# A decoder step with matrix products in seven parts: reading PSUM sums between the products of an accumulation, and another order of the seven products

## The chip, the cores and the metric

The kernel runs on one core of one Trainium2 chip. The metric is the device time of one execution in microseconds; the time before is the median of three runs. One further execution was profiled, and every duration below that is not a run's time comes from it. TensorE does the matrix products (PE, with its weight loads as PEld), VectorE (DVE), ScalarE (ACT) and GpSimd (POOL) the element-wise work; SyncE (SP) and GpSimd issue the DMAs. Products end in PSUM, out of which VectorE and ScalarE read them.

## The reference

One inference step of a decoder layer for 1024 prompt tokens and 8 sample tokens (1032 columns), everything in float32: a projection into pooling and convolution branches, an output projection, cross attention over 256 memory tokens, and a SwiGLU, each added to the residual, and a last normalisation. What matters here is the SwiGLU, with D_MODEL 1024 and D_FF 2816:

```python
    h = rmsnorm(x, g_ffn)
    x = x + (jax.nn.silu(h @ w_gate) * (h @ w_up)) @ w_down
```

## The kernel before

Columns of activations are tokens, partitions are channels. D_FF is cut into 22 tiles of 128, which the code counts with `f` and which are called values 0 to 21 here. Each float32 operand is split into a high and a low float32r part, and each product runs three passes (`PASSES`: high by high, high by low, low by high).

**Gates and values.** For one value the kernel computes two results (gate and up) for two halves of the tokens (`TH` = 516 columns), over two halves of the 1024 input channels: a product of 2 x 2 by 2 x 2 blocks. It is done as seven block products instead of eight, by sums of blocks made beforehand on both sides. On the token side the seven operands A11, A12, A22, S1, S2, S3, S4 lie in SBUF, split, for the whole stage (`ab`, 14 buffers). On the weight side `gate_prep` splits the gate weights (`wG`), and `sums_prep` forms four differences and sums (`ta`, `tb`, L1266) of the raw weights (`gr`, two loads a value) and splits them and the up weights (`wTa`, `wTb`, `wU`). A split is a high part on ScalarE or GpSimd (L363, L365) and a low part on VectorE or GpSimd (L374). A block product is `product` (L1288): 4 channel tiles x 3 passes x 2 column pieces of 258 are 24 matmuls (L1307) into one PSUM buffer. Three buffers are used in turn: two wide ones of the tag `mm` (both column pieces under one read of 516 columns), and one narrow pair of the tag `ms` (two reads of 258).

The results are sums over several products. They are formed in SBUF, in the tile `su` of a value: `copy_sums` (L1326) copies a product out with ScalarE, `plus_sums` (L1322) adds one to a quarter of `su` with VectorE. `first_two`, `sixth` and `others` (L1373 to L1412) do this in the order A11, S2, A12, S3, S1, A22, S4; for the values 0 and 1 (`AHEAD` = 2) A11 and A12 come first, since their other weights come later. S1 is read twice. So a value has one copy by ScalarE and seven additions by VectorE. Between them stand `gated` (times the token factor `Rf`, SiLU, times `Rf`; L1348, L1355), `times_value` (gate times up) and, for every second value up to 15, `combine` (L1330), which forms the seven operands of the w_down product from two neighbouring values. These go to DRAM (`hb`); values 16 to 21 go to DRAM as they are (`hd`).

**The w_down product.** `down(u)` runs for 16 units: 4 quarters `c` of the first 16 values by 4 pairs `p` of output tiles, again as seven block products, of 2 channel tiles each: 12 matmuls into one PSUM buffer. The weights of a unit come by `dn_load` and `dn_prep` (raw `dr`, sums `dt`, split into `dV` for S1, S2, S3, A22 and `dW` for A11, A12, S4), the operands by `down_blocks` (`hs`, split into `hb`), four of the seven blocks of a quarter after the first by an accumulating DMA (L385, L392). The order is `DOWN_ORDER`, which decides too which blocks are loaded first. Each product is added by VectorE to one or two of six quarters of sums (four in `x2`, two in `pp`); in the first quarter two of these start as copies by ScalarE. `both` adds quarters to one another. A last stage (`last_down`, tiles `fd`, L1606) adds the values 16 to 21 and `final` normalises.

**The order of work.** The code lists tasks; `Program.order` places them on the engines once, when the program is built, by costs per engine, by the order in which they were listed, and by the number of buffers of each tag (3 `raw`, 2 `w`, 3 `scr`, 19 `op`, 2 `mm`, 2 `ms`). Each engine then works through its own list in that order, so an instruction that waits holds up all that stand behind it on that engine.

Of the kernel before, what the change touches and what calls it, by code (L numbers as in the profile page):

```python
# [11 lines left out]
ALU = mybir.AluOpType  # L12
# [61 lines left out]
DOWN_ORDER = (A11, S2, A12, S3, S1, A22, S4)  # L74
# [178 lines left out]
def hybrid_step_kernel(ctx: ExitStack, tc: tile.TileContext, io):  # L253
# [1034 lines left out]
    def product(w, cols, xs, steps=1):  # L1288
# [4 lines left out]
        state["products"] += 1  # L1293
        if i % 3 < 2:
# [8 lines left out]
        def emit(e, js):  # L1303
            for j in js:
                for p, (wi, xi) in enumerate(PASSES):
                    for c in range(2):
                        e.matmul(bank(c), w[:, wi, cols(j)], xs[0](j, xi)[:, c * TQ : (c + 1) * TQ],  # L1307
                                 start=j == 0 and p == 0, stop=j == nj - 1 and p == 2)
# [25 lines left out]
    def of_tokens(w, col, b, steps=1):  # L1334
        return product(w, lambda j: slice(col + j * P, col + (j + 1) * P),
                       (lambda j, p: block(b, j, p), [[bkey(b, j, p) for p in range(2)] for j in range(4)]), steps)
# [36 lines left out]
    def first_two(f, between=lambda: None):  # L1373
        G = gu_w[f][0]
        su[f] = op_buf(f"su{f}", (P, 4, TH))
        copy_sums(part(f, 1), (su[f], 1), of_tokens(G, 0, A11, 4 if f < AHEAD else 1))
        between()
        plus(f, 1, 0, of_tokens(G, 512, A12, 4 if f < AHEAD else 1))
# [5 lines left out]
    def others(f):  # L1384
# [6 lines left out]
        gated(f, 1)  # L1391
        if f < FIRST_LAST and f % 2 == 0:
            he[f] = scr(f"he{f}", (P, 2, TH))
        k, e = su[f], f - 1
        second = f < FIRST_LAST and f % 2
        times_value(f, 1)
        if second:
# [3 lines left out]
        plus(f, 2, 2, of_tokens(U, 0, S4))  # L1401
        times_value(f, 0)
        if second:
# [5 lines left out]
        else:  # L1409
            dma(lambda: hd[f - FIRST_LAST], lambda: su[f][:, 0:2].rearrange("p h n -> p (h n)"), 4 * P * T,  # L1410
                r=[(k, 0), (k, 1)], w=[("hd", f)])

# [60 lines left out]
    def down(u):  # L1473
        c, p = u // 4, u % 4
        W, V = dn_w.pop(u)
        if not c:
# [3 lines left out]
            both(p, 2, 2, 4, ALU.subtract)  # L1480

        def of_hidden(b, w, cols, wkeys):
            o = db[c, b]
            return product(w, cols, (lambda j, x: o[:, x, j], [[(o, 0), (o, 1)] + wkeys] * 2))

        def plain(b, col):
            W_part = [(W, x, 0 if col(1) < 512 else 1) for x in range(2)]
            return of_hidden(b, W, lambda j: slice(col(j), col(j) + P), W_part)

        def summed(b, q):  # L1490
            return of_hidden(b, V, lambda j: slice((2 * q + j) * P, (2 * q + j + 1) * P), [])
# [7 lines left out]
        first = plain(A11, lambda j: 2 * j * P)  # L1499
        into(3, first, True)  # L1500
        into(0, first)
        into(3, summed(S2, 2))
        into(0, plain(A12, lambda j: (2 * j + 1) * P))
        into(5, summed(S3, 3), True)
        into(4, summed(S1, 0))
        into(1, summed(A22, 1))
        if c == CHUNKS - 1:
# [279 lines left out]
```

## Time and profile before

| | us |
|---|---|
| median of three runs | 1253.48 (1253.13 to 1254.77) |
| the profiled execution | 1253.93 |
| its span, first to last instruction | 1252.2 |
| gates and values, within the span | 560 to 1001 |
| w_down, within the span | 1001 to 1171 |
| last stage, within the span | 1171 to the end |

The mean granted TensorE clock was 0.994. In the rows of the profile, a group or a timeline row has line, engine, operation, output tile <- input tiles with the buffer numbers left out, the shape, and the count. A number in brackets at the end of a timeline row is the idle time of that engine just before it, with the instruction that ended it. Matmul ends are modelled, so a row of TensorE reaches some tenths of a microsecond into the next one's start.

### The profile page before, as it was taken

The page shows a single profiled execution, that of the slowest core. Times are in us where ns is not written, and L with a number is a line of the kernel's source. Part 1 is how long each engine was busy: PE and PEld are TensorE (multiplying, and loading weights), DVE is VectorE, ACT ScalarE, POOL GpSimd, SP SyncE. Part 2 cuts the span into 40 slices and gives each one's busy share as a digit, 9 for nine tenths or more (in the row PEclk, how much of TensorE's full clock was granted, in tenths as well). Part 3 has the DMA queues.
Part 4 walks back from the last instruction along what each step waited for, and adds up shares of the span by engine and source line. Part 5 has one row for each costly group of instructions (what it writes and reads, how often), then busy time and mean ns, then how long its engine had stood idle before and what let it go on. Part 6 is the DMA issues. An engine that isn't in the chain of part 4 may idle for free.

```text
span 1252.2 us, 22041 instructions
## 1 busy us (share of the span) xinstructions
PE 1217.0 (97%) x8946; PEld 1191.6 (95%) x8946; DVE 928.5 (74%) x1548; ACT 516.3 (41%) x715; POOL 481.8 (38%) x428
## 2 busy tenths in 40 slices
PE   8999989999999999999999999999999999999997
PEld 7999977999999889989999999999999999999996
DVE  7899997756267785688878668776776887768644
ACT  6766755444224534452322222222322254423533
POOL 3587682322100112205241433133321667778301
PEclk9999999999999999999999999999999999999999
DMA  7445787437465764321323133313313597666812
GB/s 280 101 87 133 172 249 207 167 117 225 139 228 163 232 267 133 118 102 60 110 102 111 60 114 116 111 60 110 119 68 119 203 304 205 183 175 186 185 54 83
DMA packets 59877, 186.48 MB, mean 149 GB/s; under 512 B 8000, under 2 KB 11776, under 8 KB 58496
## 3 DMA queue, kind: packets, MB, share of 16 engines
q1 hardware_dynamic: 52288, 157.74, 35.8%
q0 software_dynamic: 7488, 27.34, 12.2%
q8 instruction: 70, 1.15, 0.4%
q14 instruction: 31, 0.25, 0.1%
HBM read 151.42 MB, written 33.64 MB: 148 GB/s over the span
## 4 chain that ended last, share of the span: by engine, by line
PE 49%; DVE 3%; DMA 1%; issue 1%; POOL 0%; ACT 0%; DVEq 0%; SPq 0%; ACTq 0%; POOLq 0%
PE pr L1307 44%; PE fd L1606 6%; DMA dr<-in_w_dn 1%; DVE hb L374 1%; DVE x L1322 1%; DMA hs<-hb 0%; DVE dW L374 0%; POOL dt L1448 0%; DVE su L1348 0%; DVE dV L374 0%; DVE pp L1330 0%; DVE x L1658 0%; DVE pp L1322 0%; DVE dt L1448 0%; PE fin_ps L1637 0%
## 5 line engine op out<-in xcount | busy, mean ns | idle before, releaser
L1322 DVE TENSOR_TENSOR su<-pr,su 128x258 f32<-128x258 f32 (+1 forms) x204 | 109.5, 559 | 78.1 <-PE pr L1307 74.6
L1307 PE MATMUL pr<-ab,wG 128*128 128x258 f32 x1056 | 136.1, 286 | 3.1 <-ACT wG L363 1.3
L1307 PEld LDWEIGHTS pr<-ab,wG 128*128 128x128 f32 x1056 | 131.5, 192 | 4.1 <-ACT wG L363 1.4
L1307 PE MATMUL pr<-ab,wTa 128*128 128x258 f32 x1056 | 133.5, 283 | 0.0
L1307 PE MATMUL pr<-ab,wTb 128*128 128x258 f32 x1056 | 130.9, 283 | 0.0
L1307 PEld LDWEIGHTS pr<-ab,wTa 128*128 128x128 f32 x1056 | 129.7, 189 | 0.0
L1307 PEld LDWEIGHTS pr<-ab,wTb 128*128 128x128 f32 x1056 | 128.8, 190 | 0.0
L471 PE MATMUL ps<-xop,w 128*128 128x344 f32 x720 | 113.9, 320 | 0.0
L471 PEld LDWEIGHTS ps<-xop,w 128*128 128x128 f32 x720 | 113.3, 188 | 0.0
L1307 PE MATMUL pr<-hb,dV 128*128 128x258 f32 x768 | 98.6, 284 | 2.9 <-DVE x L1322 2.2
L1307 PEld LDWEIGHTS pr<-hb,dV 128*128 128x128 f32 x768 | 95.0, 190 | 3.7 <-issue 1.2
L471 PE MATMUL ps<-xq,w 128*128 128x344 f32 x576 | 94.2, 321 | 0.0
L471 PE MATMUL po<-oo,w 128*128 128x344 f32 x576 | 91.0, 320 | 0.4 <-DVE oo L1080 0.4
L471 PEld LDWEIGHTS po<-oo,w 128*128 128x128 f32 x576 | 90.7, 188 | 0.7 <-DVE oo L1080 0.7
L471 PEld LDWEIGHTS ps<-xq,w 128*128 128x128 f32 x576 | 90.6, 188 | 0.1
L1322 DVE TENSOR_TENSOR x<-pr,x 128x516 f32<-128x516 f32 (+1 forms) x122 | 63.6, 556 | 21.9 <-PE pr L1307 20.3
L1307 PE MATMUL pr<-hb,dW 128*128 128x258 f32 x576 | 74.8, 283 | 3.2 <-DVE x L1322 1.8
L675 DVE SCALAR_TENSOR_TENSOR cacc<-glu,vec,cacc 128x511 f32<-128x511 f32 (+14 forms) x116 | 76.8, 744 | 0.0
L1307 PEld LDWEIGHTS pr<-hb,dW 128*128 128x128 f32 x576 | 71.5, 189 | 3.7 <-DVE x L1322 2.0
L1606 PE MATMUL fd<-ho,w 128*128 128x258 f32 x576 | 70.0, 283 | 0.8 <-DVE x L1322 0.8
L1606 PEld LDWEIGHTS fd<-ho,w 128*128 128x128 f32 x576 | 69.4, 189 | 1.0 <-ACT w L385 1.0
L1307 PE MATMUL pr<-ab,wU 128*128 128x258 f32 x528 | 67.4, 284 | 0.0
(328 smaller groups left out, 2317.4 us busy)
## 6 DMA issues: line engine op xcount, KB each, us to landing
gr<-in_w_gu SPq DMA_DIRECT2D x44, 512.0 KB, 3.4
hs<-hb SPq DMA_DIRECT2D x28, 516.0 KB, 3.5
hb<-su SPq DMA_DIRECT2D x8, 1032.0 KB, 4.6
dr<-in_w_dn SPq DMA_DIRECT2D x16, 512.0 KB, 7.0
hb<-hb POOLq DMA_DIRECT2D x12, 516.0 KB, 8.3
spcache_k<-in_cache_k SPq DMA_DIRECT2D x12, 512.0 KB, 3.7
raw<-in_w_in SPq DMA_DIRECT2D x10, 512.0 KB
w<-in_w_in POOLq DMA_DIRECT2D x9, 512.0 KB, 6.5
```

Of the source, the lines that this page charges most:

```text
L374: e.tensor_tensor(dst(1), src(), f32(dst(0)), ALU.subtract)
L471: e.matmul(ps[:, c, :CW], w[:, wi, cols], x[:, xi, c * CW : (c + 1) * CW], start=first and p == 0, stop=last and p == 2)
L675: e.scalar_tensor_tensor(acc[h][:, n:], src[:, : HALF - n], w, acc[h][:, n:], ALU.mult, ALU.add)
L1307: e.matmul(bank(c), w[:, wi, cols(j)], xs[0](j, xi)[:, c * TQ : (c + 1) * TQ], start=j == 0 and p == 0, stop=j == nj - 1 and p == 2)
L1322: from_sums(sums, "DVE", dve, lambda e, src, sl: e.tensor_tensor(as_banks(o(sl), src), src, as_banks(a(sl), src), ALU.add), [akey], [okey])
L1606: e.matmul(view(i), w[:, wi, col : col + P], hops[k][:, xi, lo + i * width // count : lo + (i + 1) * width // count], start=(k == 0 and p ...
```

## The change

Some sums are now formed in PSUM. `product` gets `onto`: the matmuls of a product go on adding into a buffer that holds an earlier product (`start=False`), after that buffer was read. A new function `seven` replaces `first_two`, `sixth` and `others` for the values 2 to 21. It runs A11, A12, S2, S1, S3, S4, A22. A11 is copied out by ScalarE; S2 goes onto it, and their sum is copied out; S3 goes onto that, and the sum is added to the copy of S1; A22 goes onto that, and this sum is one of the results as it stands, so VectorE multiplies it by `Rf` as it reads it. S4 goes onto S1. A12 alone keeps the narrow pair. So a value has three copies by ScalarE, three additions by VectorE and one multiplication out of PSUM. Each buffer is wanted again after one product in between. The combinations and stores of a value now follow its last product (`to_hidden`).

In `down` the same is done with S2 onto A11 and S4 onto S1, in the order A11, A12, S1, S2, S3, S4, A22. A subtraction of quarters at the start of each pair goes, `second_half` and the additions of the last quarter use other quarters, and the count of buffers is stepped over (`state["products"] += 1`) so that each buffer has two products between its uses.

```diff
-DOWN_ORDER = (A11, S2, A12, S3, S1, A22, S4)
+DOWN_ORDER = (A11, A12, S1, S2, S3, S4, A22)
...
-    def product(w, cols, xs, steps=1):
+    def product(w, cols, xs, steps=1, onto=None, narrow=None):
...
-        state["products"] += 1
-        if i % 3 < 2:
+        if onto is None and narrow is None:
+            state["products"] += 1
+            narrow = i % 3 == 2
+        if onto is not None:
+            sums = onto
+        elif not narrow:
...
-                                 start=j == 0 and p == 0, stop=j == nj - 1 and p == 2)
+                                 start=onto is None and j == 0 and p == 0, stop=j == nj - 1 and p == 2,
+                                 skip_group_check=onto is not None)
...
+    def seven(f):
+        G, U, Ta, Tb = gu_w[f]
+        su[f] = op_buf(f"su{f}", (P, 4, TH))
+        k = su[f]
+        one = of_tokens(G, 0, A11, narrow=False)
+        copy_sums(part(f, 0), (k, 0), one)
+        plus(f, 0, 0, of_tokens(G, 512, A12, narrow=True))
+        gated(f, 0)
+        of_tokens(Ta, 0, S2, onto=one)
+        copy_sums(part(f, 2), (k, 2), one)
+        two = of_tokens(Tb, 0, S1, narrow=False)
+        copy_sums(part(f, 3), (k, 3), two)
+        of_tokens(Ta, 512, S3, onto=one)
+        plus(f, 3, 3, one)
+        of_tokens(U, 0, S4, onto=two)
+        plus(f, 2, 2, two)
+        start_kept(f)
+        times_value(f, 0)
+        of_tokens(Tb, 512, A22, onto=one)
+        o = part(f, 1)
+        from_sums(one, "DVE", dve, lambda e, src, sl: e.tensor_tensor(
+            as_banks(o(sl), src), src, as_banks(Rf[:, TH + sl.start : TH + sl.stop], src), ALU.mult), RF, [(k, 1)])
+        add({"ACT": act(TH)}, lambda e: e.activation(o(), o(), AF.Silu), [(k, 1)], [(k, 1)], func=AF.Silu)
+        times(f, 1, lambda: Rf[:, TH:], RF)
+        times_value(f, 1)
+        to_hidden(f)
...
-            both(p, 2, 2, 4, ALU.subtract)
...
         first = plain(A11, lambda j: 2 * j * P)
+        into(0, first)
+        into(0, plain(A12, lambda j: (2 * j + 1) * P))
+        fifth = summed(S1, 0)
+        into(4, fifth)
+        summed(S2, 2, first)
         into(3, first, True)
-        into(0, first)
-        into(3, summed(S2, 2))
-        into(0, plain(A12, lambda j: (2 * j + 1) * P))
+        state["products"] += 1
         into(5, summed(S3, 3), True)
-        into(4, summed(S1, 0))
+        plain(S4, lambda j: 512 + j * P, fifth)
+        into(2, fifth)
+        state["products"] += 1
+        if c == CHUNKS - 1:
+            both(p, 2, 2, 3)
         into(1, summed(A22, 1))
...
-        both(p, 3, 3, 5)
-        both(p, 1, 1, 3)
+        both(p, 5, 3, 5)
+        both(p, 1, 1, 5)
         both(p, 3, 4, 5)
...
         if f < AHEAD:
             sixth(f)
+            others(f)
         else:
-            first_two(f, lambda: sixth(f))
-        others(f)
+            seven(f)
```

The orders on TensorE, VectorE, ScalarE, GpSimd and SP are the same up to value 1. VectorE's order within value 7 (in the rows, `su7` is this value's tile, `pr` a PSUM buffer, `wG8`, `wTb8`, `ta9`, `tb9` weights of the next two values), before, from the read of S2 to the second multiplication by `Rf`:

```order
L1322 TENSOR_TENSOR su7_6873<-pr52_6908,su7_6873 128x516
L1322 TENSOR_TENSOR su7_6873<-pr53_0_6939,su7_6873 128x258
L1322 TENSOR_TENSOR su7_6873<-pr53_1_6940,su7_6873 128x258
L1266 TENSOR_TENSOR ta9_6999<-gr9_1_6966 128x512
L1266 TENSOR_TENSOR ta9_6999<-tb9_6997,gr9_1_6966 128x512
L1322 TENSOR_TENSOR su7_6873<-pr54_6970,su7_6873 128x516
L1322 TENSOR_TENSOR su7_6873<-pr53_0_6939,su7_6873 128x258
L1322 TENSOR_TENSOR su7_6873<-pr53_1_6940,su7_6873 128x258
L1322 TENSOR_TENSOR su7_6873<-pr55_7002,su7_6873 128x516
L374 TENSOR_TENSOR wU8_7060<-gr8_1_6717,wU8_7060 128x512
L1348 TENSOR_TENSOR su7_6873<-su7_6873,Rf_5298 128x516
```

The same in the changed kernel, where `pr14_6772` holds A11 and then S2, S3 and A22, and `pr14_6870` S1 and then S4, from the split of wG8 on:

```order
L374 TENSOR_TENSOR wG8_6858<-gr8_0_6554,wG8_6858 128x1024
L374 TENSOR_TENSOR wTb8_6863<-tb8_6734,wTb8_6863 128x1024
L1354 TENSOR_TENSOR su7_6830<-su7_6830,Rf_5298 128x516
L1266 TENSOR_TENSOR tb9_6922<-gr9_1_6868,gr9_0_6770 128x512
L1266 TENSOR_TENSOR ta9_6924<-gr9_1_6868 128x512
L1266 TENSOR_TENSOR ta9_6924<-tb9_6922,gr9_1_6868 128x512
L1266 TENSOR_TENSOR tb9_6922<-gr9_0_6770,ta9_6924 128x512
L1328 TENSOR_TENSOR su7_6830<-pr14_6772,su7_6830 128x516
L1328 TENSOR_TENSOR su7_6830<-pr14_6870,su7_6830 128x516
L1354 TENSOR_TENSOR su7_6830<-su7_6830 128x516
L1445 TENSOR_TENSOR su7_6830<-pr14_6772,Rf_5298 128x516
```

Four reads of sums are left of seven, and the read of S3 (the row with `pr14_6772` and `su7` on both sides) stands behind the four differences and sums of value 9's weights, of which two stood on VectorE in value 7 before.

ScalarE's order around value 7 before (L1326 is the copy, L1355 SiLU, L363 high parts):

```order
L1326 ACTIVATE su7_6873<-pr49_6812 128x516
L363 ACTIVATE wTb8_6906<-tb8_6775 128x1024
L1355 ACTIVATE su7_6873<-su7_6873 128x516
L363 ACTIVATE wTa9_7028<-ta9_6999 128x1024
L363 ACTIVATE wU8_7060<-gr8_1_6717 128x512
L1355 ACTIVATE su7_6873<-su7_6873 128x516
```

And now (L1332 the copy, L1361 and L1447 SiLU):

```order
L1332 ACTIVATE su7_6830<-pr14_6772 128x516
L363 ACTIVATE wG8_6858<-gr8_0_6554 128x1024
L363 ACTIVATE wTb8_6863<-tb8_6734 128x1024
L1361 ACTIVATE su7_6830<-su7_6830 128x516
L1332 ACTIVATE su7_6830<-pr14_6772 128x516
L1332 ACTIVATE su7_6830<-pr14_6870 128x516
L363 ACTIVATE wU8_6977<-gr8_1_6653 128x512
L363 ACTIVATE wTa9_7009<-ta9_6924 128x1024
L1447 ACTIVATE su7_6830<-su7_6830 128x516
```

The copies of S2's and S1's sums have come in behind the first SiLU.

VectorE's order at the end of the first quarter of w_down before (`x2_3` and `pp1` hold sums of unit 3, `x2_0` of unit 4; `hb1_` are blocks of the second quarter):

```order
L1322 TENSOR_TENSOR x2_3_10456<-pr175_10586,x2_3_10456 128x516
L1322 TENSOR_TENSOR x2_3_10456<-pr176_0_10604,x2_3_10456 128x258
L1322 TENSOR_TENSOR x2_3_10456<-pr176_1_10605,x2_3_10456 128x258
L374 TENSOR_TENSOR dW4_10599<-dr4_10439,dW4_10599 128x256
L374 TENSOR_TENSOR hb1_3_10618<-hs1_3_10297,hb1_3_10618 128x1032
L374 TENSOR_TENSOR hb1_1_10636<-hs1_1_10358,hb1_1_10636 128x1032
L374 TENSOR_TENSOR hb1_2_10654<-hs1_2_10384,hb1_2_10654 128x1032
L1322 TENSOR_TENSOR x2_3_10456<-pr177_10623,x2_3_10456 128x516
L1322 TENSOR_TENSOR pp1_10193<-pr179_0_10659,pp1_10193 128x258
L1322 TENSOR_TENSOR x2_3_10456<-pr180_10680,x2_3_10456 128x516
L1322 TENSOR_TENSOR pp1_10193<-pr179_1_10660,pp1_10193 128x258
L1322 TENSOR_TENSOR x2_3_10456<-pr181_10698,x2_3_10456 128x516
```

And now:

```order
L1328 TENSOR_TENSOR x2_3_10288<-pr35_0_10393,x2_3_10288 128x258
L1328 TENSOR_TENSOR x2_3_10288<-pr35_1_10394,x2_3_10288 128x258
L1328 TENSOR_TENSOR x2_3_10288<-pr36_10413,x2_3_10288 128x516
L1328 TENSOR_TENSOR pp1_10025<-pr37_10432,pp1_10025 128x516
L374 TENSOR_TENSOR hb1_1_10461<-hs1_1_10234,hb1_1_10461 128x1032
L1487 TENSOR_TENSOR dt5_10410<-dt5_10410,dr5_10311 128x256
L1328 TENSOR_TENSOR x2_3_10288<-pr37_10432,x2_3_10288 128x516
L1487 TENSOR_TENSOR dt5_10410<-dr5_10311,dt5_10410 128x256
L374 TENSOR_TENSOR dW5_10515<-dr5_10311,dW5_10515 128x512
L1328 TENSOR_TENSOR x2_3_10288<-pr41_0_10501,x2_3_10288 128x258
L1328 TENSOR_TENSOR x2_3_10288<-pr41_1_10502,x2_3_10288 128x258
L1328 TENSOR_TENSOR x2_0_9863<-pr42_10523,x2_0_9863 128x516
```

Of the three splits of blocks between the reads one is left on VectorE; the two others stand on GpSimd.

42 lines of the change are left out of this document (19 added, 23 removed).

## Prediction

> **What bounds the kernel now.** I read the page first, then the chain of waits in order of time, then TensorE's timeline for its gaps, and last what stands in front of each gap. The page's first section:
>
> ```profile
> span 1252.2 us, 22041 instructions
> PE 1217.0 (97%) x8946; PEld 1191.6 (95%) x8946; DVE 928.5 (74%) x1548; ACT 516.3 (41%) x715; POOL 481.8 (38%) x428
> ```
>
> TensorE is busy for 97% of the span, so the change cannot earn what it takes off VectorE; it can earn only TensorE's gaps, in the stages it touches. In the chain of waits in order of time (start, length, work) the stage of gates and values is one piece:
>
> ```profile
> 560.15 428.60 PE pr L1307 x3548
> ...
> 1001.26 6.05 PE pr L1307 x48
> ...
> 1171.11 38.55 PE fd L1606 x318
> ```
>
> For 428.60 us TensorE waits for nothing. The gaps lie from the last value to the first `fd` product. TensorE's timeline shows them in brackets at the row's end, with the instruction that ended each:
>
> ```profile
> 1001.26 1.69 PE L1307 MATMUL pr<-hb,dW 128*128 128x258 f32 x12 [0.95 <-DVE su L1322]
> ...
> 1007.98 3.19 PE L1307 MATMUL pr<-hb,dV 128*128 128x258 f32 x24 [0.69 <-ACT pp L1326]
> ...
> 1043.50 3.15 PE L1307 MATMUL pr<-hb,dW 128*128 128x258 f32 x24 [1.80 <-DVE x L1322]
> ...
> 1070.82 4.57 PE L1307 MATMUL pr<-hb,dV 128*128 128x258 f32 x36 [1.04 <-DVE x L1322]
> ...
> 1085.91 3.13 PE L1307 MATMUL pr<-hb,dW 128*128 128x258 f32 x24 [0.41 <-DVE pp L1322]
> ...
> 1134.51 3.07 PE L1307 MATMUL pr<-hb,dV 128*128 128x258 f32 x23 [0.52 <-DVE x L1322]
> ...
> 1154.15 4.60 PE L1307 MATMUL pr<-hb,dV 128*128 128x258 f32 x36 [0.64 <-DVE x L1322]
> ...
> 1171.11 38.55 PE L1606 MATMUL fd<-ho,w 128*128 128x258 f32 x318 [0.78 <-DVE x L1322]
> ```
>
> Together 0.95 + 0.69 + 1.80 + 1.04 + 0.41 + 0.52 + 0.64 + 0.78 = 6.83 us. Every releaser is an instruction that reads a sum out of PSUM: TensorE wants the buffer back. That is all there is to win, 0.5% of the span. The two stages by windows (length, busy time of PE, PEld, DVE, ACT, POOL, then clock, DMA share, GB/s):
>
> ```profile
> 560.15:988.76 428.61, 428.61 (x3550) 428.61 (x3551) 322.06 (x456) 116.02 (x157) 142.72 (x92) 1.00 0.27 96
> 1001.20:1171.10 169.90, 163.97 (x1344) 162.56 (x1345) 135.95 (x215) 77.24 (x98) 130.19 (x113) 1.00 0.78 212
> ```
>
> The first row gives 428.61 / 3550 x 24 = 2.90 us for a product of gates and values, and the second 163.97 / 1344 x 12 = 1.46 us for one of the w_down stage. The clock is full in both.
>
> **Gates and values (values 2 to 21).** The number of matmuls stays. Reads of sums by VectorE go from seven to four for a value and ScalarE's copies from one to three; one of VectorE's four now multiplies, and replaces a multiplication of SBUF by SBUF. VectorE's price is in the page's fifth section (line, tiles, count, busy time, mean ns, then idle time before):
>
> ```profile
> L1322 DVE TENSOR_TENSOR su<-pr,su 128x258 f32<-128x258 f32 (+1 forms) x204 | 109.5, 559 | 78.1 <-PE pr L1307 74.6
> L1322 DVE TENSOR_TENSOR x<-pr,x 128x516 f32<-128x516 f32 (+1 forms) x122 | 63.6, 556 | 21.9 <-PE pr L1307 20.3
> ```
>
> VectorE already waits 74.6 us for TensorE in front of the first group, so time taken off it here brings nothing: this part's gain is 0. What it can cost is new waits. Before, a buffer was wanted again three products later, two products of cover. Now S2 goes onto the sum of A11, S3 onto that of S2, S4 onto S1's, A22 onto S3's, and the next value's A11 into S4's buffer, each after one product, 2.90 us. The timeline of one value prices these steps:
>
> ```profile
> 760.76 0.60 ACT L1326 ACTIVATE su<-pr 128x516 f32<-128x516 f32 x1 [1.68 <-PE pr L1307]
> ...
> 763.46 3.07 PE L1307 MATMUL pr<-ab,wG 128*128 128x258 f32 x24
> ...
> 763.60 0.76 DVE L1322 TENSOR_TENSOR su<-pr,su 128x258 f32<-128x258 f32 x2
> ...
> 766.57 0.70 DVE L1322 TENSOR_TENSOR su<-pr,su 128x516 f32<-128x516 f32 x1 [2.21 <-PE pr L1307]
> ...
> 767.91 1.22 DVE L374 TENSOR_TENSOR wG<-gr,wG 128x1024 fp32r<-128x1024 f32 x1
> 768.03 0.64 ACT L1355 ACTIVATE su<-su 128x516 f32<-128x516 f32 x1 [0.35 <-DVE su L1348]
> ...
> 769.16 10.72 SPq L353 DMA_DIRECT2D gr<-in_w_gu  x2
> ...
> 769.45 1.06 ACT L363 ACTIVATE wTb<-tb 128x1024 fp32r<-128x1024 f32 x1 [0.78 <-PE pr L1307]
> ...
> 770.61 1.23 DVE L374 TENSOR_TENSOR wTb<-tb,wTb 128x1024 fp32r<-128x1024 f32 x1 [0.27 <-ACT wTb L363]
> ...
> 772.99 0.69 DVE L1266 TENSOR_TENSOR tb<-gr,gr 128x512 f32<-128x512 f32 x1
> 773.60 0.68 DVE L1266 TENSOR_TENSOR ta<-gr 128x512 f32<-128x512 f32 x1
> ...
> 782.88 0.33 SPq L353 DMA_DIRECT2D hb<-su  x1
> ...
> 785.00 1.06 ACT L363 ACTIVATE wTb<-tb 128x1024 fp32r<-128x1024 f32 x1 [3.48 <-DMA hb<-su]
> ```
>
> A read starts 0.14 us after the next product does (763.46, 763.60) and takes 0.60 on ScalarE or 0.70 on VectorE, so 2.90 - 0.14 - 0.70 = 2.06 us of slack stand behind each. I follow the tightest one, S3's read in an odd value, in the order of VectorE shown above, with its A11 starting at 0. A12 ends at 5.8; its two halves are read until 6.7; multiplication 7.3; wG split 1.22 to 8.5; wTb split 1.23 to 9.8, its ScalarE half ready by then (5.8 + 1.06 + 1.06 = 7.9); multiplication 10.4. The four differences need the raw weights: SP issues that load once the wG split has freed its buffer, at 8.5, and the row above used such a load 772.99 - 769.16 = 3.83 us after issue, so they start at 12.3 and take 4 x 0.61 (772.99 to 773.60): 14.8. S3 ends at 4 x 2.90 + 2.90 = 14.5, so its read runs to 15.5, and A22 wants the bank at 17.4: 1.9 us to spare. The ScalarE copies: S2's sum is whole at 8.7, ScalarE has then done wG (6.9), wTb (8.0) and the SiLU (8.7). Its copy runs to 9.3, and S3 wants the bank at 11.6: 2.3 to spare. The row at 785.00 shows what can eat into it: wTb waited for the store of the value before, issued at 782.88, and landed 2.12 later. By the new order that store follows A22's read (0.84), the wTa split (1.22) and three SBUF operations of 0.61, 3.9 in all, and lands at 6.0, before wTb's turn at 6.9; for the last six values, whose store is twice the size, I allow a wait of 1 us, still inside 2.3. The stores to hb keep their places on SP between the two raw loads. So the stage stays at 428.6 us: 0, bounded by nothing below (no gap to win), and above by what a late load does, which the rivals price.
>
> Here a rule of the Trainium skill speaks against the change: Perfetto Trace Analysis, section Optimizing Tensor Performance, says that "Independent matmul groups should rotate through different PSUM banks", so that reading one sum overlaps the next group. By it, going back to the bank just read gives that overlap up. The rows decide how much: one product still stands between, and 0.84 us of read fit into its 2.90. The sum by the rule is among the rivals.
>
> **The w_down stage.** Sixteen units of seven products. VectorE's reads go from 6 to 5 in the four units of the first quarter and from 8 to 7 in the others: 4 x 6 + 12 x 8 = 120 before, 104 now. Beside the page's group of x stands that of pp, from the groups of the stage:
>
> ```profile
> L1322 DVE TENSOR_TENSOR pp<-pr,pp 128x258 f32<-128x258 f32 (+1 forms) x38 | 20.0, 548 | 8.4 <-PE pr L1307 8.4
> ```
>
> (63.6 + 20.0) / 120 = 0.70 us a read, so 16 reads are 11.2 us of VectorE's 135.95, and eight sums of quarters (L1330) go too. TensorE does not become shorter by it; the gaps may. The sums that are added onto are wanted again after two products, as before. The gaps one by one.
>
> The gap of 1.80 at 1043.50: in the timeline in front of it stand three splits of the next quarter's blocks,
>
> ```profile
> 1037.21 4.49 PE L1307 MATMUL pr<-hb,dV 128*128 128x258 f32 x36
> ...
> 1037.70 5.14 DVE L374 TENSOR_TENSOR hb<-hs,hb 128x1032 fp32r<-128x1032 f32 x3
> ...
> 1042.76 0.68 DVE L1322 TENSOR_TENSOR x<-pr,x 128x516 f32<-128x516 f32 x1
> ```
>
> 5.14 us in which no sum is read, against 2 x 1.46 = 2.92 of cover. In the new order one of the three is left there and two are on GpSimd: a third of 5.14 is 1.71, inside the cover. I take 1.65 of 1.80 as gone, and at 1085.91, the same place a quarter later, 0.35 of 0.41. At the seam (1001.26, 0.95) VectorE's last reads of value 21 now have a product of cover and the first w_down products take other buffers: 0.95 gone. The 0.69 behind it is a ScalarE copy queued after block splits; the queue stays, two thirds gone, 0.45. The four others (1.04, 0.52, 0.64, 0.78; sum 2.98) stand behind weight splits and loads that stay, of which one read fewer a unit removes a part between none and all; I take 45%, 1.35. Sum: 1.65 + 0.35 + 0.95 + 0.45 + 1.35 = 4.75 us.
>
> Against it, every engine's order from value 2 on is new, and new orders make new gaps. Their cost is bounded by 0 and by the present gaps again, 6.83; the mean present gap, 6.83 / 8 = 0.85 us, is what I put in, one such gap. Net 4.75 - 0.85 = 3.9 us. The products' order itself I cost at nothing: V, the last weights to be prepared, is wanted third instead of second, one product (1.46 us) later; dW's second piece is wanted sixth instead of seventh, and is split a unit ahead. The blocks are loaded in their new order of use, four of seven through an accumulating DMA as before, so SP's and GpSimd's DMAs keep their number and size.
>
> **Rivals.** (a) The gaps stay: what holds VectorE up is splits and loads, not the reads, and gaps move rather than go. For it: the 1.04 gap follows a slow raw load; against it: the largest gap, 1.80, has its reads behind splits that leave VectorE. Time 1253.5; chance 0.20. (b) All eight gaps go and none comes: 1253.48 - 6.83 = 1246.6; chance 0.06, for the trace ties only part of the 6.83 to the reads. (c) Slower: the raw load is late, and with VectorE's queue blocked on it the read of S3 misses A22. It decides from 1.9 us of lateness on, that is a load of over 5.7 us. The page's sixth section (count, KB, median us to landing) and the chain hold the bounds:
>
> ```profile
> gr<-in_w_gu SPq DMA_DIRECT2D x44, 512.0 KB, 3.4
> ...
> dr<-in_w_dn SPq DMA_DIRECT2D x16, 512.0 KB, 7.0
> ```
>
> ```profile
> 1049.50 9.87 DMA dr<-in_w_dn
> ```
>
> At 3.4 there is no wait; at the 7.0 of the crowded stage each value loses 7.0 - 5.7 = 1.3 us. If half of the twenty values do, 13 us go, less the 3.9 gained: 1253.48 + 9.1 = 1262.6. The DMA share of 0.27 in this stage speaks against it; chance 0.10. (d) The reads are laid bare: TensorE stands still while each sum that it goes on adding to is read, 5 sums x 20 values x (0.14 + 0.70) = 84 us, so 1337.5; chance 0.02, since the order puts a product between. This is what the rule of Perfetto Trace Analysis in the Trainium skill would come to here. That the change does not do what it says is excluded by the order of instructions.
>
> **The numbers.** The forecast has the rest, 0.62. The profiled execution took 1253.93, of which 1252.2 are the span; 1253.93 - 3.9 = 1250.03, and the median of the runs lies 0.45 below that execution: 1249.6 us. The range of 8 in 10: below, all gaps gone, 1246.6; above, (a) and on top one new gap of 1.04, the largest but one: 1254.5. About 0.2% (2.5 us, to 1251.0) is what a measurement of this kernel can tell from no change. Of the forecast's 0.62 I give 0.54 to gains over 2.5 us and 0.08 to smaller ones, so faster 0.54 + 0.06 = 0.60; same 0.08 + 0.20 less 0.01 for a loss past the line = 0.27; slower 0.10 + 0.02 + 0.01 = 0.13.
>
> **What would show it.** Right: the chain again has one unbroken TensorE piece of about 428 us for gates and values; VectorE's and ScalarE's PSUM reads stay at 0.70 and 0.60; the gap after the first quarter of w_down is under 0.3 us and the gaps from the seam to the first fd product sum to about 3 us instead of 6.83. Wrong: any gap before `pr` of an S2, S3, S4 or A22 in the gate stage with a PSUM read as its releaser (then the cover of one product fails), or gaps in w_down that still sum to 6 us or more (then reads were not what held VectorE up).

## The result, and the profile after

| | before | after |
|---|---|---|
| median, six runs each on one chip | 1253.31 us | 1244.73 us (1244.0 to 1250.05) |
| ratio of the runs, 95% interval | | 0.9936 (0.9913 to 0.9958) |
| profiled execution, its span | 1253.93, 1252.2 | 1247.84, 1246.0 |
| gates and values to the first fd product (chain) | 560.15 to 1171.11 = 610.96 | 559.45 to 1164.64 = 605.19 |
| first fd product to the end | 81.09 | 81.36 |

The changed kernel is faster by 0.6%, 8.6 us between the medians and 6.1 between the two profiled executions; of the latter 610.96 - 605.19 = 5.77 lie between the start of gates and values and the first `fd` product. The forecast was 3.9, and the measured median lies below the range.

The first section of the page after:

```profile
span 1246.0 us, 21884 instructions
PE 1217.0 (98%) x8946; PEld 1191.4 (96%) x8946; DVE 877.4 (70%) x1459; ACT 536.4 (43%) x745; POOL 420.1 (34%) x386
```

TensorE's busy time is what it was (1217.0), VectorE's is 51.1 us shorter, ScalarE's 20.1 longer. Between these two profiles the gain is idle time of TensorE alone. The chain of waits in order of time (start, length, work):

```profile
559.45 460.77 PE pr L1312 x3812
...
1046.24 9.43 DMA dr<-in_w_dn
...
1055.80 0.42 DVE dt L1487
1056.22 0.62 DVE x L1328
...
1056.88 107.75 PE pr L1312 x888
1164.64 38.57 PE fd L1646 x318
```

The unbroken piece now reaches past the seam. TensorE's timeline has two gaps left of the eight:

```profile
1026.29 1.91 PE L1312 MATMUL pr<-hb,dV 128*128 128x258 f32 x12 [0.31 <-DVE x L1328]
...
1056.88 3.17 PE L1312 MATMUL pr<-hb,dV 128*128 128x258 f32 x24 [0.73 <-DVE x L1328]
```

0.31 + 0.73 = 1.04 us instead of 6.83. Both end with a read of a sum, and the second read stands behind `dt`, which waited for a raw load of 9.43 us. The reads themselves, in the groups of the page (count, busy time, mean ns, idle time before):

```profile
L1328 DVE TENSOR_TENSOR su<-pr,su 128x516 f32<-128x516 f32 (+1 forms) x98 | 52.8, 559 | 92.4 <-PE pr L1312 92.2
L1332 ACT ACTIVATE su<-pr 128x516 f32<-128x516 f32 (+1 forms) x63 | 37.3, 594 | 83.0 <-PE pr L1312 83.0
```

These means mix wide and narrow reads. By form, a wide read of `su` took 692 ns on VectorE before and after, a wide copy 603 ns on ScalarE before and 601 after. In front of the reads of `su` VectorE waits 92.2 us for TensorE, 74.6 before: part of the time taken off it there became waiting.

### The profile page after: what moved, and what is told of

It reads as the page before. It is cut to its first block, busy times and chain, and to the rows that moved or that the text cites. A ratio compares the mean times of both kernels' runs of the same rounds, so it can differ in the third digit from the quotient of the medians.

```text
span 1246.0 us, 21884 instructions
## 1 busy us (share of the span) xinstructions
PE 1217.0 (98%) x8946; PEld 1191.4 (96%) x8946; DVE 877.4 (70%) x1459; ACT 536.4 (43%) x745; POOL 420.1 (34%) x386
## 4 chain that ended last, share of the span: by engine, by line
PE 51%; DMA 2%; DVE 1%; POOL 0%; ACT 0%; issue 0%; DVEq 0%; POOLq 0%; SPq 0%; ACTq 0%
PE pr L1312 46%; PE fd L1646 6%; DMA dr<-in_w_dn 2%; DMA hs<-hb 0%; POOL hb L374 0%; POOL dV L374 0%; DVE x L1698 0%; PE fin_ps L1677 0%; DVE ab L376 0%; DVE x L1328 0%; DVE xss L401 0%; DVE wG L374 0%; ACT dV L363 0%; ACT hb L385 0%; DVE Rf_m L503 0%
## 5 line engine op out<-in xcount | busy, mean ns | idle before, releaser
L1312 PE MATMUL pr<-ab,wG 128*128 128x258 f32 x1056 | 133.3, 286 | 2.8 <-ACT wG L363 1.0
L1312 PE MATMUL pr<-ab,wTb 128*128 128x258 f32 x1056 | 134.0, 283 | 0.0
L374 POOL TENSOR_TENSOR wU<-gr,wU 128x512 fp32r<-128x512 f32 x22 | 34.9, 1585 | 252.4 <-ACT wU L363 252.2
L1328 DVE TENSOR_TENSOR su<-pr,su 128x516 f32<-128x516 f32 (+1 forms) x98 | 52.8, 559 | 92.4 <-PE pr L1312 92.2
L1328 DVE TENSOR_TENSOR x<-pr,x 128x258 f32<-128x258 f32 (+1 forms) x102 | 53.8, 552 | 28.8 <-PE pr L1312 28.2
L1332 ACT ACTIVATE su<-pr 128x516 f32<-128x516 f32 (+1 forms) x63 | 37.3, 594 | 83.0 <-PE pr L1312 83.0
```

The lines of the kernel that those rows point to most:

```text
L374: e.tensor_tensor(dst(1), src(), f32(dst(0)), ALU.subtract)
L1328: from_sums(sums, "DVE", dve, lambda e, src, sl: e.tensor_tensor(as_banks(o(sl), src), src, as_banks(a(sl), src), ALU.add), [akey], [okey])
L1332: from_sums(sums, "ACT", lambda n: act(n, True), lambda e, src, sl: e.activation(as_banks(o(sl), src), src, AF.Copy), [], [okey])
```

## Experiments

Theory A is the prediction's: reads of sums, and splits in the same queue, keep PSUM buffers from TensorE, so fewer reads close gaps. There are eighteen runs besides the first two. The table has what the sections below draw on: the ratio to the kernel before on the same chip, and from each profile the time from the first w_down product to the first `fd` product, the time from there to the end, their sum, and the idle time of TensorE in its timeline's brackets from the last value into the `fd` products (985 to 1180 us). The times are between rows of the timeline, which start up to 0.2 us ahead of the chain's pieces.

| kernel | ratio (95%) | w_down | last | sum | idle |
|---|---|---|---|---|---|
| before | | 169.85 | 81.09 | 250.9 | 6.83 |
| before again | 0.9992 (0.9974 to 1.0010) | 170.14 | 81.13 | 251.3 | 5.54 |
| after | 0.9936 (0.9913 to 0.9958) | 164.77 | 81.52 | 246.3 | 1.04 |
| after again | 0.9955 (0.9935 to 0.9975) | 164.31 | 81.46 | 245.8 | 1.33 |
| gates only | 0.9998 (0.9981 to 1.0016) | 172.54 | 81.82 | 254.4 | 8.55 |
| w_down only | 0.9943 (0.9925 to 0.9961) | 163.51 | 81.47 | 245.0 | 0.94 |
| reads back | 0.9967 (0.9951 to 0.9982) | 165.31 | 82.88 | 248.2 | 2.60 |
| before, no subtraction | 1.0001 (0.9988 to 1.0013) | 169.41 | 81.19 | 250.6 | 5.34 |
| gates only, no subtraction | 0.9942 (0.9923 to 0.9961) | 164.70 | 81.10 | 245.8 | 2.28 |
| after, with subtraction | 0.9981 (0.9963 to 1.0000) | 167.59 | 81.57 | 249.2 | 3.65 |
| products' and blocks' order | 0.9963 (0.9944 to 0.9981) | 166.48 | 82.89 | 249.4 | 4.38 |
| products' order only | 0.9971 (0.9954 to 0.9988) | 164.46 | 82.95 | 247.4 | 4.10 |
| blocks' order only | 0.9993 (0.9975 to 1.0010) | 171.65 | 81.53 | 253.2 | 6.14 |
| A12 and S2 exchanged | 1.0012 (0.9999 to 1.0024) | 170.23 | 81.28 | 251.5 | 5.43 |
| new order, S1 second | 0.9981 (0.9968 to 0.9995) | 165.80 | 83.07 | 248.9 | 4.43 |
| buffers rotated | 0.9997 (0.9982 to 1.0013) | 170.52 | 81.54 | 252.1 | 5.60 |

Every edit lets the planner place all later instructions anew, so each kernel stands for its edit and its plan together. The changed w_down gave sums of 244.2 to 248.2 in six profiles, with three kernels of the last two parts of this section (in one of these a product of gates and values, 2.90 us, stands behind the first of w_down and is taken off); a difference of that size between two profiles alone shows no cause.

### Both kernels again

No edit; a second timing and profile of each.

> The kernel before, timed and profiled a second time, to see how far one profiled execution stands for the runs. Theory A (the whole gain is the gaps of TensorE from the seam to the first fd product, 6.83 us before and 1.04 after; the 2.8 us that the medians differ by beyond that are the spread of single executions): the gaps sum to 6.3 to 7.3 us again, a median of 1251 to 1254. Theory B (something outside these gaps is faster too, such as the granted clock): the gaps sum to the same, but the span of this profile and that of the changed kernel's second profile differ by 8 us or more.

> The changed kernel a second time. Theory A: the gaps from the seam to the first fd product sum to 0.8 to 1.5 us again, the chain has one piece through gates and values, and the two second profiles differ in span by 5 to 7 us; the medians by 6 to 9. Theory B: the spans differ by 8 us or more, and the difference beyond the gaps lies in a stage where the mean granted clock differs by more than 0.002.

Measured: medians 1253.06 and 1246.65; spans 1249.4 and 1244.4, 5.0 apart; idle 5.54 and 1.33 us, the first below the 6.3 to 7.3 that were expected. Gates and values have no gap after the change. Theory A's description of where the gain lies holds: in the profiles w_down and what follows are 4.6 to 5.5 us shorter. The rest of the 8.6 us of the first medians did not come again (6.2 here, 1246.65 against 1252.82, the median of all runs of before on that chip).

### Each half alone

Gates only: the changed kernel with `down` and `DOWN_ORDER` of before. W_down only: the changed kernel with the old gates.

```diff
-DOWN_ORDER = (A11, A12, S1, S2, S3, S4, A22)
+DOWN_ORDER = (A11, S2, A12, S3, S1, A22, S4)
```

```diff
-            seven(f)
+            first_two(f, lambda: sixth(f))
+        others(f)
...
+    state["products"] += 1
```

> Gates and values as in the changed kernel, w_down in its old form (old order, no accumulation, all 120 reads). Theory A: gates and values have no gap to win, so only the seam's 0.95 and part of the 0.69 go: 1 to 2 us faster than before, gaps of w_down 5 us or more. Rival (the stage of gates and values carries half of the gain or more, through VectorE time that it frees for w_down's first quarter): 4 us faster or more, w_down's gaps 3 us or less.

> Gates and values in their old form, w_down as changed (new order, accumulation, 104 reads), the rotation of buffers in w_down as in the changed kernel. Theory A: 4 to 5 of the 5.8 us of gaps go: 4 to 7 us faster than before, gaps of w_down 2 us or less and the seam's gap still there. Rival (half or more comes from gates and values): 3 us faster or less.

Gates only gains nothing, 0.9998, where 1 to 2 us were expected. W_down only has the whole gain: 0.9943, and of the gaps of before only the seam's is left, with another of 0.19:

```profile
1002.02 3.28 PE L1312 MATMUL pr<-hb,dW 128*128 128x258 f32 x24 [0.75 <-DVE su L1328]
```

So with the changed w_down the seam's gap goes by the change of gates and values, as predicted. It can go another way: with the old gates and the buffers rotated (below) there is none at the seam either, but one of 1.98 us 8 us later. Gates only, for its part, has a gap of 7.35 us in w_down, which before did not have. Its chain of waits:

```profile
1017.34 16.68 DMA x<-x2d
1034.02 2.09 issue
1036.11 0.20 DVE x L1336
1036.31 0.41 issue
1036.72 0.43 DVE pp L1328
...
1037.19 4.67 PE pr L1312 x24
```

A read of `pp` stands on VectorE behind a subtraction (L1336) of two quarters of sums, and that behind a load of `x`. It is the subtraction at the start of each pair that the change removes from w_down.

### The subtraction

Taken out of before and out of gates only, put into the changed kernel; in all three the sums of w_down are not the reference's.

```diff
-            both(p, 2, 2, 4, ALU.subtract)
```

> The kernel before, with the subtraction of two quarters of sums at the start of a pair left out (so the sums of w_down are not the reference's); nothing else changes but the places that the order gives to what is left. Theory A (reads, and splits in the same queue): the gaps stay at 5 to 7 us and the time within 1.5 us of before. Rival S (the subtraction, which waits for the loads of x and stands in VectorE's queue ahead of reads, is what holds the buffers): gaps of 3 us or less, 3 us faster or more.

> The kernel with only gates and values changed, again without the subtraction at the start of a pair (sums of w_down not the reference's). In its profile with the subtraction the gap of 7.35 us at 1037 stood behind a subtraction that the trace ties to a load of x of 16.68 us. Rival S: that gap goes, the gaps sum to 3 us or less, 4 us faster or more than with it. Theory A: the gap moves to another read, gaps of 4 us or more, within 2 us of before.

> The changed kernel with the subtraction of two quarters put back at the start of each pair (the sums of w_down are then not the reference's). Rival S: w_down grows from 164.5 to 168 us or more, with a gap behind a VectorE instruction that waits for a load of x; 3 us slower than the changed kernel or more. Rival O and theory A: below 166.5 us, within 2 us of the changed kernel.

Out of gates only, the gap goes and 8.6 us of the sum (254.4 to 245.8) with it, against theory A, which had the gap move to another read. Into the changed kernel, it makes one gap of 3.65 us, and the sum goes from 246.3 to 249.2. The chain there is plain:

```profile
1023.13 13.44 DMA x<-x2d
...
1036.59 0.04 DVE x L1336
...
1037.21 0.70 DVE x L1328
...
1037.95 7.16 PE pr L1312 x46
```

Out of before, it changes nothing (1.0001, idle 5.34), as theory A expected. So the subtraction is not what made the gaps of before; it is a trap that the old form carries: in the two profiles with these gaps it waits for a load of x of 16.68 or 13.44 us. The changed w_down does not have it.

### Reads or order

Reads back: the changed kernel, S2 and S4 read and added on their own.

```diff
-        summed(S2, 2, first)
         into(3, first, True)
-        state["products"] += 1
+        into(3, summed(S2, 2))
...
-        plain(S4, lambda j: 512 + j * P, fifth)
         into(2, fifth)
-        state["products"] += 1
+        into(2, plain(S4, lambda j: 512 + j * P))
```

The products' and blocks' order: before with the new `DOWN_ORDER` and the products listed by it. Then each of the two alone.

```diff
         first = plain(A11, lambda j: 2 * j * P)
         into(0, first)
         into(3, first, True)
         into(0, plain(A12, lambda j: (2 * j + 1) * P))
         into(4, summed(S1, 0))
         into(3, summed(S2, 2))
         into(5, summed(S3, 3), True)
...
         into(2, plain(S4, lambda j: 512 + j * P))
...
         into(1, summed(A22, 1))
```

> The changed kernel, but in w_down S2 and S4 are not added onto A11 and S1 in PSUM: each is read and added by VectorE, in the new order of products (9 reads a unit, 7 in the first quarter: 136 instead of 104, 22.4 us more of VectorE by 0.70 a read). Theory A (fewer reads of sums give TensorE its buffers back sooner): gaps between the seam and the first fd product of 4 us or more, 3 to 8 us slower than the changed kernel. Rival O (the new order of products and blocks, and the subtractions that went, make the gain; the reads do nothing): gaps of 2 us or less, within 2 us of the changed kernel.

> The kernel before, in which only the seven products of w_down and the blocks come in the new order; all 120 reads, no accumulation, the subtraction kept. Rival O (the new order makes the gain): w_down from its first product to the first fd product takes 165 to 166 us instead of 169.9, 4 us faster or more. Rival S (order and the missing subtraction together are needed): 168 us or more for that stage, within 2 us of before.

> The kernel before, with only the seven products of w_down in the new order; the blocks are loaded in the old order. If it is the products' order that counts (the sums V of the weights are wanted third instead of second, and three products on V stand in a row): w_down 167 us or less, 3 to 5 us faster than before, as with both. If it is the blocks' order: w_down 169 us or more, within 2 us of before.

> The kernel before, with only the blocks of w_down loaded in the new order (and so S1 by accumulating DMA instead of S3); the products in the old order. If it is the blocks' order that counts: w_down 167 us or less, 3 to 5 us faster than before. If it is the products' order: w_down 169 us or more, within 2 us of before or slower, since blocks come in an order other than that of their use.

With 32 reads more, 136 and thus more than before, w_down still takes 165.31; its last stage is 1.4 longer. Its ratio of 0.9967 stands 0.1 to 0.3% above the changed kernel's two, 1.5 to 3.9 us, with intervals that overlap: what the reads are worth is not told from nothing. Theory A expected 4 us of gaps or more and got 2.60, of which 1.24 lie in the last stage and end with loads (0.42 with `ho`, 0.82 with `w`), not with a read. The order of the products alone, with all 120 reads and the subtraction, brings w_down from 169.85 to 164.46; with the blocks' order 166.48; the blocks' order alone shortens nothing (171.65). Both ratios, 0.9971 and 0.9963, have intervals below 1. What the order alone does not bring is the end. The timeline of products' order only:

```profile
999.39 3.14 PE L1307 MATMUL pr<-hb,dW 128*128 128x258 f32 x24 [0.97 <-DVE su L1322]
1006.53 1.73 PE L1307 MATMUL pr<-hb,dW 128*128 128x258 f32 x12 [1.10 <-DVE pp L1322]
...
1168.45 6.79 PE L1606 MATMUL fd<-ho,w 128*128 128x258 f32 x54 [1.54 <-DVE x L1322]
```

The gap of 1.54 within `fd` stands behind sums of quarters, in the chain:

```profile
1164.00 3.78 DVE x L1330
1167.79 0.62 DVE x L1322
```

The changed kernel, with fewer reads and fewer such sums, has no gap there, and its last stage is 81.5 instead of 82.95. Before, in the old order, has all reads and sums too and a last stage of 81.09, so it is the new order with all of them that lengthens it.

### What in the order

Before with A12 ahead of S2 and nothing else (the diff), and the products' order only with S1 ahead of A12; then before with the buffers' count moved on by one ahead of w_down (`state["products"] += 1`).

```diff
+        into(0, plain(A12, lambda j: (2 * j + 1) * P))
         into(3, summed(S2, 2))
-        into(0, plain(A12, lambda j: (2 * j + 1) * P))
```

> The kernel before with one exchange in the order of w_down's products: A12 ahead of S2, so that the weights' sums V are wanted third instead of second; the rest as before. If the gain of the new order is the later use of V: w_down 167 us or less, 3 us faster or more. If it is another feature of it: w_down 169 us or more, within 2 us of before.

> The kernel with only the products in the new order, but with S1 moved ahead of A12, so that V is wanted second again. If the gain is the later use of V: w_down 169 us or more, within 2 us of before. If it is another feature of the order (which sums are read with which, where S4 and A22 stand): w_down 166.5 us or less, 3 us faster or more.

> The kernel before with the count of buffers moved on by one ahead of w_down, so that the narrow pair falls to other products, as in the kernels with only gates and values changed. Rival R (which product has the narrow pair sets the gaps): w_down takes 165 to 166 us instead of 169.9, 4 us faster or more. All others: 168 us or more, within 2 us of before.

My first idea, that V is wanted third and no longer second, falls: with A12 ahead of S2 nothing is gained (170.23), and with V second again w_down is still 165.80, though the end's gap (1.55) leaves less of it in the time, 0.9981. Nor is it which product has the narrow pair: 170.52. What is left are the places of S1, S4 and A22, and the order of A11's two reads, which the products' order exchanges too. Which of these, the runs do not tell; and gates only without the subtraction reaches 164.70 in the old order, so the new order is one way to such a plan and not the only one.

What the plans have in common, the traces show. In the five profiles of kernels with the old gates, the subtraction and S1 behind S3 (before twice, blocks' order only, A12 and S2 exchanged, buffers rotated), VectorE splits weights and blocks for 6 to 8.6 us without a read at the end of the first quarter, and the gap behind it is 1.80 to 3.26 us. In the three with the products in one of the new orders and all reads, the reads come between the splits, and the longest such stretch there is 2.7 to 2.9 us, with a gap of 0.37 to 0.81 behind it. Products' order only:

```profile
1033.96 1.52 DVE L374 TENSOR_TENSOR hb<-hs,hb 128x1032 fp32r<-128x1032 f32 x1 [0.17 <-ACT hb L363]
...
1037.27 1.72 DVE L374 TENSOR_TENSOR hb<-hs,hb 128x1032 fp32r<-128x1032 f32 x1
```

Before has three such splits in one row of 5.14 us there. So the long gap goes with splits in front of reads, as the prediction had it, and the order alone takes them out of the way. By which step the planner comes to it is not shown, nor that the length of the stretch alone decides: the changed kernel has one of 5.1 us (1036.58 to 1041.64) and no gap behind it.

### The cover of one product

The changed kernel with this listing, and the same with its products tied to it by a key:

```diff
-        one = of_tokens(G, 0, A11, narrow=False)
-        copy_sums(part(f, 0), (k, 0), one)
-        plus(f, 0, 0, of_tokens(G, 512, A12, narrow=True))
+        plus_a12 = of_tokens(G, 512, A12, narrow=True)
+        copy_sums(part(f, 0), (k, 0), plus_a12)
+        one = of_tokens(G, 0, A11, narrow=False)
+        plus(f, 0, 0, one)
...
-        of_tokens(Ta, 512, S3, onto=one)
-        plus(f, 3, 3, one)
         of_tokens(U, 0, S4, onto=two)
         plus(f, 2, 2, two)
+        of_tokens(Ta, 512, S3, onto=one)
+        plus(f, 3, 3, one)
```

```diff
-                ..., [k for _, _, k in sums])
+                ..., [k for _, _, k in sums] + ([] if narrow is None and onto is None else [("row",)]))
```

> The changed kernel, but in gates and values the order is A12, A11, S2, S1, S4, S3, A22, so that S2, S4 and A22 go onto a sum straight after it, with no product between: 3 reads a value for 20 values. Theory A (the cover of one product is what makes the accumulation free): each of the 60 lays bare 0.14 + 0.70 or 0.60 and some queueing, 0.85 to 2 us, so 50 to 120 us slower than the changed kernel, with gaps before these products whose releaser is the read. Rival (the read is hidden by TensorE working ahead on the other bank of the pair): under 15 us slower.

> In the kernel with the order A12, A11, S2, S1, S4, S3, A22 the planner had put another product between each pair again, so no read lay bare. Here the products are tied to that order, so S2, S4 and A22 do follow a sum's read directly, and A22 of one value and A11 of the next have the narrow product between. Theory A (the cover of one product is what makes the accumulation free): 60 bare reads of 0.85 to 2 us, 50 to 120 us slower than the changed kernel. Rival (TensorE does not wait for the whole read): under 15 us slower.

In the first the planner put other products between, the accumulations kept their cover, and gates and values had no gap: 0.9964. It tells nothing of bare reads. The second took 1321.68 us, 1.0542 (1.0497 to 1.0586); gates and values took 509.71 us, 69.45 more than after. Nineteen values by windows, after (values 3 to 21) and here (from the third product of value 2 to that of value 21):

```profile
615.56:999.71 384.15, 384.15 (x3194) 384.15 (x3193) 251.87 (x351) 122.04 (x169) 60.32 (x37) 1.00 0.31 106
```

```profile
613.31:1057.47 444.16, 399.81 (x3192) 387.93 (x3192) 271.46 (x336) 131.74 (x193) 29.57 (x23) 1.00 0.24 84
```

A value takes 444.16 / 19 = 23.38 us instead of 384.15 / 19 = 20.22, so each of its three bare reads costs 1.05: the gaps are 0.86, 0.69 and 0.79, 0.78 idle in the mean, and 0.27 is time in which TensorE counts as busy. The 60 reads make 63 of the 69.45 us; the rest has one gap of 3.59 us ahead of value 2 (at 603.99) and a clock of 0.50 behind it. One of the bare reads in the timeline, S3's and then A22:

```profile
1000.18 0.70 DVE L1328 TENSOR_TENSOR su<-pr,su 128x516 f32<-128x516 f32 x1 [0.28 <-PE pr L1312]
...
1000.93 3.17 PE L1312 MATMUL pr<-ab,wTb 128*128 128x258 f32 x24 [0.79 <-DVE su L1328]
```

The read takes 0.70 and the gap 0.79. With one product between, the same reads cost nothing. That is how far the rule of the Trainium skill goes (Perfetto Trace Analysis, section Optimizing Tensor Performance: groups should rotate through PSUM banks so that reads overlap the next group): the runs agree that a read without another group beside it is laid bare, and show that here one group of 2.90 us is rotation enough.

### A late load

Each raw load of gates and values from value 2 on is issued twice into the same buffer, in both kernels; every engine keeps its order.

```diff
-            dma(lambda raw=raw: raw[:], lambda i=i: io["w_gu"][2 * f + i], 4 * P * D, w=[(raw,)])
+            add({"SP": 0.05}, lambda e, raw=raw, i=i: [e.dma_start(raw[:], io["w_gu"][2 * f + i]) for _ in range(1 if f < AHEAD else 2)], (), [(raw,)], nbytes=4 * P * D)
```

> The changed kernel with each raw load of gates and values from value 2 on issued twice into the same buffer, so that the second one lands 7.2 us or more after the first one's issue (3.6 each); the planned order of every engine is the same. Rival c of the prediction (from 5.7 us on the read of S3 misses A22): 1.5 us or more for half of the twenty values, gates and values 15 us longer or more, with gaps before A22 or S3. Otherwise (more slack than was worked out): under 3 us longer.

> The kernel before with the same doubled loads. If two products of cover make it more tolerant of a late load than one: gates and values longer by half of what the changed kernel loses or less. If the loss comes from the weights themselves, which arrive too late for their products in both: the same loss in both, within 3 us.

The changed kernel takes 1282.42 us, 1.022 (1.0186 to 1.0253) of before, with a gap in most odd values, where rival (c) put it. One of them in its chain:

```profile
677.53 3.46 DMA gr<-in_w_gu
...
681.01 3.49 DMA gr<-in_w_gu
...
684.59 0.69 DVE tb L1266
685.28 1.21 DVE ta L1266 x2
...
687.13 0.70 DVE su L1328
...
687.87 8.84 PE pr L1312 x71
```

Landed 6.97 us after issue, then the four differences, then S3's read, then A22, 1.39 late by the timeline's bracket. By the prediction's bound of 5.7 it would be 1.27. But before loses far more: 1333.24, 1.0625 (1.0590 to 1.0659), gates and values 518.26 instead of 441.11 us, against 476.15 instead of 440.26 after. The expectation that two products of cover bear more than one is wrong, and so is its rival, the same loss in both: the old form loses 77 us, the new one 36. Of the 77, 54 are idle time of TensorE and 23 longer busy time at a granted clock of 0.95 in this stage; of the 36, 26 and 10 at 0.98 (below). That the old form's idle time comes of more reads queued behind the same differences is what its timeline suggests and no run shows.

## Why the prediction was wrong in size

- *Gates and values gain nothing.* Right: 0.9998 for this half alone, and no gap in its stage.
- *The reads keep 0.70 and 0.60, and one product covers them.* Right; without it each costs 1.05, of which 0.78 idle, where rival (d) had 0.84.
- *The seam's 0.95 goes.* Right, and with the changed w_down by the gates' half.
- *"The products' order itself I cost at nothing."* This is the step that failed. The order alone shortens w_down by 169.85 - 164.46 = 5.4 us in the profiles; the last stage gives 82.95 - 81.09 = 1.9 of it back, and the whole is 0.3% shorter (0.9971). In the sum's own terms, 4.75 of old gaps were to go and 0.85 to come, 3.9 net; 6.83 went and 1.04 came, 5.79 net, which is the 5.77 of the two chains.
- *"That is all there is to win", and the range's lower end of 1246.6 from it.* Too tight: the first median, 1244.73, lies 1.9 below, the second, 1246.65, on it.
- *"One read fewer a unit removes a part", 45% of the four gaps (1.35 us).* Mis-sized, and put on a cause that w_down does not need. All four went, and with more reads than before it still takes 165.31. The prediction put all four behind weight splits and loads; the one of 0.78 stood behind sums of quarters (2.22 us at 1168.14 in the chain of before). In the new order with all reads the last stage takes 1.4 to 1.9 us longer than before's or the changed kernel's; by the ratios (0.9963 to 0.9971 against 0.9936 to 0.9955) fewer reads and sums are worth 1 to 4 us on top of the order, with intervals that overlap.
- *The gap of 1.80, by two splits that leave VectorE.* It went, as forecast. In five traces such a gap stands behind a long stretch of splits, and the order alone shortens that; the splits were not moved by themselves.
- *Eight sums of quarters go, priced at nothing.* Four of the eight are the subtraction. True of before (1.0001), not of the changed kernel, where these four put back cost about 3 us.
- *One new gap, 0.85.* The two left sum to 1.04; but charged on top of 2.08 us of old ones assumed to stay, it was too much. Rival (b), all gaps gone, came nearest; I gave it 0.06.
- *A gap is worth its idle time.* Too little for the longest, by the clock that follows it.
- *Rival (c).* Right in mechanism, and near in size where the loads were made late (1.39 against 1.27), but loads did not come late, and the old kernel is the more fragile.

What stays open: what it is in the places of S1, S4 and A22 or in A11's reads that makes the planner keep VectorE's queue clear, and how much of the first medians' 8.6 us beyond the profiles' 6.1 is spread; the second timing gave 6.2.

## What to carry to other kernels

When an engine works through a list in order, ask of each change to the list which long or waiting instruction it puts in front of a read that frees a buffer: here an order of products, which changed no work at all, made 0.3% by itself. Here one product of 2.90 us between a sum's read of 0.70 and its next use hid the read fully; without one each read cost 1.05. A dependence on a load that sits in front of such reads is a risk even where the profile of the day shows no wait behind it.

## What the runs showed of the hardware

A long gap costs more than itself. The same gap, in the two profiles of before, before and then before again:

```profile
1043.50 3.15 PE L1307 MATMUL pr<-hb,dW 128*128 128x258 f32 x24 [1.80 <-DVE x L1322]
```

```profile
1040.43 4.65 PE L1307 MATMUL pr<-hb,dW 128*128 128x258 f32 x24 [1.84 <-DVE x L1322]
```

The 24 matmuls take 3.15 us after the one and 4.65 after the other. The next 4.5 us by windows (the number after the bracket of POOL is the granted clock):

```profile
1043.50:1048.00 4.50, 4.50 (x37) 4.50 (x38) 3.34 (x8) 3.78 (x5) 4.41 (x4) 1.00 0.91 306
```

```profile
1040.43:1044.93 4.50, 4.50 (x25) 4.50 (x26) 1.92 (x4) 3.19 (x5) 4.13 (x3) 0.62 0.88 316
```

In the twenty profiles, from 565 us on and ahead of products of these stages, behind 116 gaps of 0.6 to 1.65 us (60 of them bare reads) the clock of the next 4.5 us was 0.98 or 1.00; behind 21 gaps of 1.68 to 2.92 it was 1.00 eleven times and 0.62 or 0.63 ten times; behind ten of 3.26 to 7.35 it was always 0.50 to 0.68. Gaps that stand close seem to count together: at the start of gates and values 17 profiles have one of 1.02 to 1.45 us and one of 0.93 to 0.97 that ends 1.7 us later (before: 1.28 and 0.96, ending at 558.44 and 560.15), and behind the second the clock was 0.62 or 0.65 nine times and 1.00 eight times. At 0.62, 0.38 x 4.5 = 1.7 us are lost behind a gap of 1.8. The Trainium skill (TensorE: Matmul & The Clock Gate, section What's actually happening) gives half the clock after an idle window of some 3.4 us, until a busy window of as long; half for 3.4 us is 0.62 over 4.5, an estimate that agrees, but the gaps at which it sets in here begin at half that length.
